# Mixer B's weighted products on GpSimd's queue: their places in a written-out plan and the tiles that they use, and one more tile for the sample's near keys

## Chip, core and metric

The kernel runs on one core of a Trainium2 chip. The metric is the device time of one execution in microseconds (us); given is the median of several runs. One further execution was recorded by the hardware profiler.

## What is computed

One step of a one-layer hybrid decoder, for a prompt of 1024 tokens and a sample group of 8 sequences with 4 new tokens each (32 rows). A normed input is projected into three mixers and their gates. Mixer A is sliding-window attention with sinks. Mixer B is attention in three groups of heads with dilations 1, 4 and 16; the three group outputs of a head slot are added, each weighted by its share of the softmax denominators:

```python
w_mix = jax.nn.softmax(jnp.stack(lses), axis=0)
ob = jnp.sum(w_mix[..., None] * jnp.stack(outs), axis=0)
```

Mixer C is a causal pooling over windows of 2, 4, 8 and 16 positions, followed by a small linear map. Each mixer's output is multiplied by a SiLU gate, projected to 1024 columns, merged by three sigmoid gates, passed through one output projection and added to the residual. The sample group does the same against key/value states of up to 2048 rows, which are inputs.

## The kernel before, in words

Everything is float32, computed as pairs of float32r numbers (a high and a low part), so each projection is three matmuls per tile of 128 input rows. TensorE runs the 58 column blocks of the input projection one after the other (`project`, L332). A block is three chunks of columns (384, 384 and 288 tokens), a chunk is 24 matmuls (L320), and after every 6 matmuls `tick` (L203) is called, so a block has 12 ticks. A chunk ends with the evacuation of its PSUM bank by ScalarE and VectorE; there are three such banks (`pj`).

All other work is hung on the ticks. A *plan* (`planned`, L219) is a list of (tick, function); at tick n all functions with that number emit their instructions. The *side* generators are advanced by a rate per tick. A tick orders instructions on each engine's queue, nothing more: an engine runs its queue in order, as soon as semaphores allow. The compiler framework hands out the buffers of a tag in the order of the first writes and adds all the waits.

The stage of this change follows the last block of the attention stage. Eight blocks (L1171 to L1176) project the gates of mixers C (t1c), B (t1_4, t1_5) and A (t1_0 to t1_3), 96 ticks. Beside them run, by `merge_plan` (L1155 to L1163):

- the weights of mixer B's groups (`stats_b`, L638): loaded into the tile `rows`, computed on VectorE, and written to DRAM (`w_scr`, L668) at tick 8;
- the pooling (`pooling`, L904): running sums (`window`) on GpSimd for the first half of the channels and on VectorE for the second, results `sa` and `sbb` in the tags l2 to l5; `body` and `small` (VectorE) turn them into `diff` in the tags df0 and df1; then `mix`, `times` and `parts_of` (ticks 22 to 39);
- mixer B's weighted products, six of them (pair p of 0, 1; group g of 0, 1, 2). Each is a load of the group's output from DRAM (`get_o`, L1118, 512 KB), two loads that spread the weights over 64 partitions each (`get_w`, L1126, 256 KB each), a product (`scale_o`, L1131), and for the second and third group a sum (`add_o`, L1136). All of these are issued from GpSimd's queue (POOL). After three groups `gate_b` (L1142, VectorE) multiplies the gate of the pair by the sum.

At ticks 48, 60, 72 and 84 the gates t1_0 to t1_3 are to be written to l2, l3, l4 and l5; their first chunk's evacuation comes four ticks later.

The sample group's attention (`sample`, L677) is a side generator. It issues its loads on SyncE's queue (SP): near keys and values into the tag `near` (two buffers, L683), far keys and values into the tag `kv` (five buffers, L711), which `rows` shares. Score steps t = 0 to 4 (L746 near, L765 far), then probabilities `probs` into tiles `pm` and `pd` (cleared by GpSimd, L802 and L804, at tick 41; filled by VectorE, L817, L822), then products with the values (L829, L852, L880). L774 and L829 are the new rows' small matmuls. The copies of the sample states in DRAM (L182) are issued on GpSimd's queue from tick 96 on.

```python
(44, get_b(1, 0, "l4")), (44, get_bw(1, 0, "l5")), (49, gate_b(0, (0, 0))),
...
(60, get_b(1, 2, "l3")), (60, get_bw(1, 2, "l5")), (67, scale_b(1, 2)), (67, add_o((1, 0), (1, 2))), (73, gate_b(1, (1, 0)))]
```

Of the kernel before, what the change touches and what calls it, by code (L numbers as in the profile page):

```python
# [7 lines left out]
F32 = mybir.dt.float32  # L8
# [7 lines left out]
L = 1024  # L16
# [80 lines left out]
def build(tc, x_p, x_s, w_in, w_pr, w_out, nw, fnw, sink, sinkrow, w_pool, pscale, st_a, st_b1, st_b2, st_b3, st_c,  # L97
# [579 lines left out]
    def sample(pl, ahead):  # L677
# [4 lines left out]
        def load_near(src):  # L682
            t = pl.tile([128, 8, 128], F32, tag="near", name="near", bufs=2)  # L683
            sp.dma_start(out=t, in_=src)
            near.append(t)

        load_near(kt_a)
        load_near(kt_b1[:, 0])
        qn = pl.tile([128, 10, 2, 32], F32, name="qn")
        pool.memset(qn, 0.0)  # L690
        for hh in range(2):
# [44 lines left out]
        for t in range(5):  # L736
            ps = bank("s")
            if t < 3:
                yield from idle(1)
                for nq in range(4):  # L740
                    for half in range(2):
                        n = 4 * half + nq
                        for p in range(2):
                            r0 = 64 * p + 32 * half
                            rhs = near[0 if t < 2 else 1 + p][:, n, :]
                            pe.matmul(ps[r0:r0 + 32, 0:128], lhsT=qm[:, 2 * t + p, half, 32 * nq:32 * nq + 32], rhs=rhs,  # L746
                                      start=(nq == 0), stop=(nq == 3))
            else:
                g = t - 2
                q_t = qd[0]  # L750
                for hh in range(2):
                    hs = slice(64 * hh, 64 * hh + 64)
                    dve.tensor_copy(out=q_t[hs].rearrange("p a b c -> p (a b) c")[:, :, 16 * hh:16 * hh + 496:33],
                                    in_=qsmp[hs, 2 * t:2 * t + 2].rearrange("p a (b t) -> p (a b) t", b=2))
                yield from idle(4)
                for nq in range(4):
                    yield from idle(4)
                    for i in range(4):
                        for half in range(2):
                            n = 4 * half + nq  # L760
                            kk = kv_tiles["k", g, n].rearrange("p (i a j) -> p i a j", i=4, a=2)
                            t16 = 4 * nq + i
                            for p in range(2):
                                r0 = 64 * p + 32 * half
                                pe.matmul(ps[r0:r0 + 32, 0:128], lhsT=q_t[:, p, half, 32 * t16:32 * t16 + 32], rhs=kk[:, i, p, :],  # L765
                                          start=(t16 == 0), stop=(t16 == 15))
                    load_ahead(4 * (g - 1) + nq + 2)
                    if nq < 3:
                        yield
            for half in range(2):  # L770
                for p in range(2):
                    r0 = 64 * p + 32 * half
                    ki = 0 if t < 2 else 2 * t - 3 + p
                    pe.matmul(ps[r0:r0 + 32, 128:160], lhsT=qn[:, 2 * t + p, half, :], rhs=ksmp[:, ki, :], start=True, stop=True)  # L774
            init = nsinkrow[:, t:t + 1] if t < 2 else 3.0e38
            dve.tensor_tensor_reduce(out=es[t], in0=ps[:, 0:160], in1=sb[:, t, :], scale=1.0, scalar=init, op0=ALU.add, op1=ALU.min,
                                     accum_out=st[:, t:t + 1])
            act.activation(out=es[t], in_=es[t], func=AF.Exp, scale=-1.0, bias=st[:, t:t + 1], accum_out=st[:, 8 + t:9 + t])
            if t < 2:
                act.activation(out=st[:, 16 + t:17 + t], in_=st[:, t:t + 1], func=AF.Exp, bias=sinkrow_sb[:, t:t + 1])  # L780
                dve.tensor_tensor(out=st[:, 16 + t:17 + t], in0=st[:, 16 + t:17 + t], in1=st[:, 8 + t:9 + t], op=ALU.add)
                dve.reciprocal(out=st[:, 16 + t:17 + t], in_=st[:, 16 + t:17 + t])
                dve.tensor_scalar(out=es[t], in0=es[t], scalar1=st[:, 16 + t:17 + t], scalar2=None, op0=ALU.mult)
            if t == 1:
                load_near(kt_b1[:, 1])
            if t == 2:
                load_near(st_a[:, 1].rearrange("n k c -> k n c"))
                load_near(st_b1[:, 1, :, 0:128].rearrange("n k c -> k n c"))
            yield
        dve.tensor_tensor(out=st[:, 24:25], in0=st[:, 2:3], in1=st[:, 3:4], op=ALU.min)  # L790
# [113 lines left out]
    def pooling(pl, up, oc, sa, sbb, after):  # L904
# [16 lines left out]
        def window(t, eng, dst, src, sh, base, hs=slice(0, 128)):  # L921
            def run():
                eng.tensor_tensor(out=dst[hs, base:n], in0=src[hs, base:n], in1=src[hs, base - sh:n - sh], op=ALU.add)
            return run

        def body(t, hh):
            hs, s = ((slice(0, 64), sa[t]), (slice(64, 128), sbb[t]))[hh]

            def run():
                dve.scalar_tensor_tensor(out=diff[t][hs, 16:L], in0=s[hs, 32:16 + L], scalar=pw_sb[hs, t, 16:17], in1=up[t][hs, 32:16 + L],  # L930
                                         op0=ALU.mult, op1=ALU.subtract)
                dve.tensor_tensor(out=diff[t][hs, 0:16], in0=s[hs, 16:32], in1=pw_sb[hs, t, 0:16], op=ALU.mult)
                dve.tensor_tensor(out=diff[t][hs, 0:16], in0=diff[t][hs, 0:16], in1=up[t][hs, 16:32], op=ALU.subtract)
            return run
# [4 lines left out]
        def small(t):  # L939
            def run():  # L940
                e = ext[:, t]
                dve.tensor_copy(out=e[:, :, 16:20], in_=usmp[:, t, :].rearrange("p (n i) -> p n i", i=4))
                win_s(ea, e, 1, 2)
                if t == 0:
                    win_s(eb, ea, 2, 4, slice(64, 128))
                else:
                    win_s(eb, ea, 2, 4)
                    win_s(ea, eb, 4, 8)
                    win_s(eb, ea, 8, 16, slice(64, 128))
                for hs, s in ((slice(0, 64), ea), (slice(64, 128), eb)):  # L950
                    dve.scalar_tensor_tensor(out=diff[t][hs, L:NT].rearrange("p (n i) -> p n i", i=4), in0=s[hs, :, 16:20],
                                             scalar=pw_sb[hs, t, 16:17], in1=e[hs, :, 16:20], op0=ALU.mult, op1=ALU.subtract)
            return run
# [27 lines left out]
        def parts_of(t):  # L981
            def run():
# [3 lines left out]

        h = slice(64, 128)
        out = [(0, setup), (1, window(0, pool, sa[0], up[0], 1, 1)), (2, window(0, pool, sbb[0], sa[0], 2, 3, h)),
               (9, window(1, dve, sa[1], up[1], 1, 1)), (11, window(1, dve, sbb[1], sa[1], 2, 3)),
               (13, window(1, dve, sa[1], sbb[1], 4, 7)), (15, window(1, dve, sbb[1], sa[1], 8, 15, h)),  # L990
               (16, body(0, 0)), (18, body(0, 1)), (19, small(0)), (20, body(1, 0)), (22, body(1, 1)), (23, small(1)),
               (30, rows_u(0)), (32, rows_u(1)), (33, times(0)), (35, parts_of(0)), (37, times(1)), (39, parts_of(1))]
        out += [(22 + 2 * ci, mix(0, c0, cn)) for ci, (c0, cn) in enumerate(CH)]
        out += [(28 + 2 * ci, mix(1, c0, cn)) for ci, (c0, cn) in enumerate(CH)]
# [139 lines left out]
    def add_o(a, b):  # L1134
        def run():
            pool.tensor_tensor(out=t_s[a][:, :L], in0=t_s[a][:, :L], in1=t_s[b][:, :L], op=ALU.add)  # L1136
        return run

    def gate_b(p, key):
        def run():  # L1140
            g = t1[4 + p][:, :L].rearrange("p (u r) -> p r u", r=8)
            dve.tensor_tensor(out=g, in0=g, in1=t_s[key][:, :L].rearrange("p (r u) -> p r u", r=8), op=ALU.mult)  # L1142
        return run

    def get_b(p, g, tag):
        return get_o((p, g), gl, tag, 4 + 2 * g + p)

    def get_bw(p, g, tag):
        return get_w((p, g, "w"), gl, tag, w_scr[g], 16 * p)

    def scale_b(p, g):
        return scale_o((p, g), (p, g, "w"))

# [1 line left out]
    merge_plan = stats_b(s1)  # L1155
    merge_plan += pooling(s1, up, oc, sa, sbb, (lambda: None, lambda: None))
    merge_plan += [
        (20, get_b(0, 0, "l2")), (20, get_bw(0, 0, "l3")), (27, scale_b(0, 0)),
        (28, get_b(0, 2, "l4")), (28, get_bw(0, 2, "l5")), (35, scale_b(0, 2)), (35, add_o((0, 0), (0, 2))),
        (36, get_b(0, 1, "l3")), (36, get_bw(0, 1, "l5")), (43, scale_b(0, 1)), (43, add_o((0, 0), (0, 1))),  # L1160
        (44, get_b(1, 0, "l4")), (44, get_bw(1, 0, "l5")), (49, gate_b(0, (0, 0))),
        (51, scale_b(1, 0)), (52, get_b(1, 1, "l3")), (52, get_bw(1, 1, "l5")), (59, scale_b(1, 1)), (59, add_o((1, 0), (1, 1))),
        (60, get_b(1, 2, "l3")), (60, get_bw(1, 2, "l5")), (67, scale_b(1, 2)), (67, add_o((1, 0), (1, 2))), (73, gate_b(1, (1, 0)))]  # L1163

    ahead = []
    smp = sample(s1, ahead)
# [351 lines left out]
```

## Time and profile before

| | us |
|---|---|
| median of 3 runs | 1084.41 (1084.41 to 1086.29) |
| profiled execution, its own time | 1083.06 |
| span of the profiled execution, first to last instruction | 1081.3 |
| TensorE busy / VectorE / ScalarE / GpSimd | 1040.3 / 433.1 / 346.6 / 215.1 |
| mean granted TensorE clock (1 is 2.4 GHz) | 0.987 |

The stage runs from about 448 to 598 us of the span. In the rows, PE is TensorE, PEld its weight loads, DVE VectorE, ACT ScalarE, POOL GpSimd, SP SyncE; "SPq", "POOLq" and "ACTq" are their queues when they issue a transfer. L12 is line 12 of the kernel.

### The profile page before, as it was taken

To read this page: it belongs to the slowest core of one execution; us is meant where nothing else is said; L and a number is where in the kernel's file an instruction comes from. 1 tells how busy PE (TensorE), PEld (TensorE's weight loads), DVE (VectorE), ACT (ScalarE), POOL (GpSimd) and SP (SyncE) were. 2 spreads that over 40 slices of the span, in tenths; PEclk is the share of its full clock that TensorE was granted. 3 is DMA by queue.
4 is the path that set the end of the run, shared out by engine and by line. 5 is a ranking of instruction groups with operands and counts; after the bars stand their busy time and mean duration, and the time that the engine had idled before them with its cause. 6 is when DMAs were issued, how large, how long until landed. Compare 5 with 4: busy or idle time off the path is not lost.

```text
span 1081.3 us, 18059 instructions
## 1 busy us (share of the span) xinstructions
PE 1040.3 (96%) x7421; PEld 992.5 (92%) x7421; DVE 433.1 (40%) x952; ACT 346.6 (32%) x890; POOL 215.1 (20%) x325
## 2 busy tenths in 40 slices
PE   7999999999999999999949999999999999999995
PEld 6998999999999999989939999999999999998884
DVE  6556654544535343475412551212112221255331
ACT  5455553544535344323201321211111121243211
POOL 5400030211303030305440340311113111121011
PEclk9999999999999999999979999999999999999998
DMA  7241242525344363488763823544234250332231
GB/s 262 87 152 57 65 132 85 168 69 174 102 156 144 111 192 100 142 269 287 212 210 105 259 98 107 177 145 136 77 118 150 65 172 20 113 112 93 79 100 41
DMA packets 54573, 144.41 MB, mean 134 GB/s; under 512 B 13030, under 2 KB 29732, under 8 KB 53156
## 3 DMA queue, kind: packets, MB, share of 16 engines
q1 hardware_dynamic: 40044, 58.94, 17.2%
q0 software_dynamic: 4640, 51.16, 14.3%
q10 hardware_dynamic: 9808, 33.17, 9.6%
q8 instruction: 58, 0.95, 0.4%
q14 instruction: 23, 0.19, 0.1%
HBM read 127.65 MB, written 60.55 MB: 174 GB/s over the span
## 4 chain that ended last, share of the span: by engine, by line
PE 84%; DMA 7%; DVE 3%; POOL 3%; ACT 2%; issue 1%; POOLq 0%; SPq 0%; ACTq 0%
PE ps_pj L320 55%; PE ps_pj L1389 5%; DMA w_in<-w_scr 5%; PE ps_s L1389 4%; PE ps_s L1254 4%; PE ps_t L1254 4%; PE ps_s L519 3%; PE ps_o L561 3%; PE ps_t L539 2%; POOL o_in L1131 1%; DMA w_raw<-in_w_in 1%; POOL o_in L1136 1%; DMA x_nat<-in_x_p 1%; PE ps_t L456 1%; DVE sq L295 1%
## 5 line engine op out<-in xcount | busy, mean ns | idle before, releaser
L320 PE MATMUL ps_pj<-xh,w_hi 128*128 128x384 f32 (+2 forms) x1408 | 461.0, 334 | 18.0 <-DVE t L1104 15.3
L320 PE MATMUL ps_pj<-xl,w_hi 128*128 128x384 f32 (+2 forms) x1408 | 444.8, 323 | 0.3 <-DVE xl L309 0.3
L320 PE MATMUL ps_pj<-xh,w_lo 128*128 128x384 f32 (+2 forms) x1408 | 443.4, 321 | 0.6 <-DVE w_lo L150 0.6
L320 PEld LDWEIGHTS ps_pj<-xh,w_hi 128*128 128x128 f32 x1408 | 262.5, 189 | 27.4 <-DVE t L1104 15.5
L320 PEld LDWEIGHTS ps_pj<-xl,w_hi 128*128 128x128 f32 x1408 | 263.0, 190 | 1.0 <-DVE xl L309 0.5
L320 PEld LDWEIGHTS ps_pj<-xh,w_lo 128*128 128x128 f32 x1408 | 261.8, 189 | 1.0 <-DVE w_lo L150 1.0
L150 DVE TENSOR_TENSOR w_lo<-w_raw,w_hi 128x1024 fp32r<-128x1024 f32 x55 | 73.7, 1339 | 203.0 <-ACT w_hi L149 202.6
L1263 ACT ACTIVATE mth<-ps_pj 128x384 f32<-128x384 f32 (+1 forms) x72 | 33.4, 464 | 255.0 <-PE ps_pj L320 252.3
L1271 POOL TENSOR_TENSOR m<-m,mth 128x384 f32<-128x384 f32 (+1 forms) x48 | 48.7, 1032 | 284.3 <-DVE mth L1269 284.0
L411 POOL TENSOR_SCALAR k<-k 64x384 fp32r<-64x384 f32 (+1 forms) x44 | 20.1, 458 | 297.5 <-ACT k L407 297.1
L526 ACT ACTIVATE e<-e,nm_b 128x256 f32<-128x256 f32 (+1 forms) x96 | 44.2, 461 | 63.1 <-DVE nm_b L523 62.8
L149 ACT ACTIVATE w_hi<-w_raw 128x1024 fp32r<-128x1024 f32 x57 | 60.1, 1054 | 0.8 <-DMA w_raw<-in_w_in 0.8
L371 DVE SCALAR_TENSOR_TENSOR q<-ps_pj,q 64x384 fp32r<-64x384 f32 (+1 forms) x60 | 30.7, 512 | 60.3 <-ACT q L370 60.2
L519 PE MATMUL ps_s<-k,q 128*128 128x256 f32 x320 | 51.6, 285 | 0.7 <-DVE nm_a L523 0.7
L519 PEld LDWEIGHTS ps_s<-k,q 128*128 128x128 f32 x320 | 45.9, 188 | 1.1 <-issue 1.0
L539 PE MATMUL ps_t<-ident,e 128*128 128x128 f32 x276 | 42.8, 273 | 1.8 <-ACT pt L544 1.1
L370 ACT ACTIVATE q<-ps_pj 64x384 fp32r<-64x384 f32 (+1 forms) x60 | 26.8, 447 | 50.4 <-PE ps_pj L320 29.3
L182 POOL DMA_DIRECT2D out_b_s<-in_st_b x84 | 42.2, 507 | 0.0
L526 ACT ACTIVATE e<-e,nm_a 128x256 f32<-128x256 f32 (+1 forms) x64 | 31.1, 487 | 28.1 <-DVE nm_a L523 28.1
L523 DVE CUSTOM_DVE_ANT_0 e<-ps_s,bias 128x256 f32<-128x256 f32 (+1 forms) x96 | 31.9, 371 | 14.9 <-PE ps_s L519 14.3
L539 PEld LDWEIGHTS ps_t<-ident,e 128*128 128x128 f32 x276 | 33.9, 140 | 4.1 <-ACT pt L544 1.7
L408 DVE TENSOR_TENSOR k<-ps_pj,k 64x384 fp32r<-64x384 f32 (+1 forms) x44 | 21.7, 494 | 38.7 <-ACT k L407 35.3
(243 smaller groups left out, 1337.5 us busy)
## 6 DMA issues: line engine op xcount, KB each, us to landing
out_b_s<-in_st_b POOLq DMA_DIRECT2D x64, 511.0 KB, 6.7
w_raw<-in_w_in ACTq DMA_DIRECT2D x55, 512.0 KB
kv<-in_kt_b SPq DMA_DIRECT2D x16, 512.0 KB
kv<-in_st_b SPq DMA_DIRECT2D x16, 512.0 KB
out_b_s<-in_st_b POOLq DMA_DIRECT2D x16, 508.0 KB, 5.2
o_scr<-os SPq DMA_DIRECT2D x20, 256.0 KB
x_nat<-in_x_p SPq DMA_DIRECT2D x8, 512.0 KB
w_raw<-in_w_pr ACTq DMA_DIRECT2D x8, 512.0 KB
```

The source lines that it names most:

```text
L149: act.activation(out=hi, in_=raw, func=AF.Copy)
L150: eng.tensor_tensor(out=lo, in0=raw, in1=hi.bitcast(F32), op=ALU.subtract)
L182: pool.dma_start(out=dst, in_=src)
L320: pe.matmul(ps[:, :cn], lhsT=parts[p][0][:, k, :], rhs=parts[p][1][:, k, c0:c0 + cn], start=(step == 0), stop=(step == 23))
L519: pe.matmul(ps[:, 256 * hd:256 * hd + 256], lhsT=q, rhs=rhs, start=(i == 0), stop=(i == 1))
L526: act.activation(out=e[:, hd, :nk], in_=e[:, hd, :nk], func=AF.Exp, scale=-1.0, bias=nm, accum_out=z)
L539: pe.transpose(tp[:, o:o + 128], e[:, hd, 128 * k:128 * k + 128], ident)
L561: pe.matmul(ps[64 * hd:64 * hd + 64, c0:c0 + 128], lhsT=v[:, tl, 64 * hd:64 * hd + 64], rhs=pt[:, o:o + 128], start=(k == 0), stop=(k == n ...
L1254: pe.matmul(pp[:, :cn], lhsT=a[:, k, :], rhs=b[k][:, c0:c0 + cn], start=(step == 0), stop=(step == last))
L1263: act.activation(out=th[:, :cn], in_=ps[:, :cn], func=AF.Tanh, scale=0.5)
L1271: pool.tensor_tensor(out=dst, in0=dst, in1=th[:, :cn], op=ALU.add)
L1389: pe.matmul(banks[c0][:rows, :cn], lhsT=a[:, k, t0:t0 + rows], rhs=wo[k][b][:, c0:c0 + cn], start=(k == 0 and si == 0), stop=(k == 7 and s ...
```

## The change

The products get other places in the plan: the first at tick 12 instead of 20, and the plan's last entry at 63 instead of 73. Within pair 0 the groups come in the order 0, 1, 2. A third product's load is under way while a second one waits for its weights, and the second and third products of pair 1 use the tags df0 and df1, which `parts_of` frees at ticks 35 and 39. `body` of the first half of the channels moves ahead of the running sums of the second. The third near-key tile no longer waits for one of the two near buffers: it takes a buffer of the tag `kv` and is loaded with the first two. The near values' loads move: st_a to t == 1, the first half of st_b1 to t == 3.

```diff
         load_near(kt_a)
         load_near(kt_b1[:, 0])
+        third = pl.tile([128, 16 + L], F32, tag="kv", name="near3", bufs=5)[:, :1024].rearrange("p (n k) -> p n k", n=8)
+        sp.dma_start(out=third, in_=kt_b1[:, 1])
+        near.append(third)
...
             if t == 1:
-                load_near(kt_b1[:, 1])
-            if t == 2:
                 load_near(st_a[:, 1].rearrange("n k c -> k n c"))
+            if t == 3:
                 load_near(st_b1[:, 1, :, 0:128].rearrange("n k c -> k n c"))
...
-               (9, window(1, dve, sa[1], up[1], 1, 1)), (11, window(1, dve, sbb[1], sa[1], 2, 3)),
-               (13, window(1, dve, sa[1], sbb[1], 4, 7)), (15, window(1, dve, sbb[1], sa[1], 8, 15, h)),
-               (16, body(0, 0)), (18, body(0, 1)), (19, small(0)), (20, body(1, 0)), (22, body(1, 1)), (23, small(1)),
+               (9, body(0, 0)), (11, body(0, 1)), (12, window(1, dve, sa[1], up[1], 1, 1)), (13, window(1, dve, sbb[1], sa[1], 2, 3)),
+               (14, window(1, dve, sa[1], sbb[1], 4, 7)), (16, window(1, dve, sbb[1], sa[1], 8, 15, h)),
+               (17, small(0)), (18, body(1, 0)), (20, body(1, 1)), (22, small(1)),
...
+    def get_d(p, g, t):
+        return get_o((p, g), s1, f"df{t}", 4 + 2 * g + p)
+
+    def get_dw(p, g, t):
+        return get_w((p, g, "w"), s1, f"df{t}", w_scr[g], 16 * p)
...
-        (20, get_b(0, 0, "l2")), (20, get_bw(0, 0, "l3")), (27, scale_b(0, 0)),
-        (28, get_b(0, 2, "l4")), (28, get_bw(0, 2, "l5")), (35, scale_b(0, 2)), (35, add_o((0, 0), (0, 2))),
-        (36, get_b(0, 1, "l3")), (36, get_bw(0, 1, "l5")), (43, scale_b(0, 1)), (43, add_o((0, 0), (0, 1))),
-        (44, get_b(1, 0, "l4")), (44, get_bw(1, 0, "l5")), (49, gate_b(0, (0, 0))),
-        (51, scale_b(1, 0)), (52, get_b(1, 1, "l3")), (52, get_bw(1, 1, "l5")), (59, scale_b(1, 1)), (59, add_o((1, 0), (1, 1))),
-        (60, get_b(1, 2, "l3")), (60, get_bw(1, 2, "l5")), (67, scale_b(1, 2)), (67, add_o((1, 0), (1, 2))), (73, gate_b(1, (1, 0)))]
+        (12, get_b(0, 0, "l2")), (12, get_bw(0, 0, "l3")), (20, scale_b(0, 0)),
+        (21, get_b(0, 1, "l3")), (22, get_bw(0, 1, "l4")), (30, scale_b(0, 1)), (30, add_o((0, 0), (0, 1))),
+        (23, get_b(0, 2, "l5")), (31, get_bw(0, 2, "l4")), (37, scale_b(0, 2)), (37, add_o((0, 0), (0, 2))), (43, gate_b(0, (0, 0))),
+        (38, get_b(1, 0, "l5")), (38, get_bw(1, 0, "l4")), (46, scale_b(1, 0)),
+        (40, get_d(1, 1, 0)), (40, get_dw(1, 1, 1)), (48, scale_b(1, 1)), (48, add_o((1, 0), (1, 1))),
+        (49, get_d(1, 2, 0)), (49, get_dw(1, 2, 1)), (57, scale_b(1, 2)), (57, add_o((1, 0), (1, 2))), (63, gate_b(1, (1, 0)))]
```

## Rows read from the trace of the kernel before

**Rows 1.** The page's granted clock in 40 slices of 27 us, tenths of full speed.

```profile
PEclk9999999999999999999979999999999999999998
```

**Rows 2.** Waits of PE, 440 to 640 us: us in total, times, longest.

```profile
PE ps_pj L320 <- DVE t L1104: 15.3, 1, 15.3
PE ps_s L746 <- DMA near<-in_kt_b: 2.5, 1, 2.5
```

**Rows 3.** The chain that ended last, 546 to 573 us: start, us, what.

```profile
546.97 12.22 DMA w_in<-w_scr
...
559.35 2.34 POOL o_in L1131
...
561.76 2.35 POOL o_in L1136
...
564.14 0.50 ACT t L1103
...
564.66 0.57 DVE t L1104
...
565.27 4.99 PE ps_pj L320 x18
```

**Rows 4.** Stretches: us; busy (count) of PE, PEld, DVE, ACT, POOL; clock, DMA share, GB/s.

```profile
460.00:465.00 5.00, 2.51 (x42) 2.26 (x41) 0.81 (x5) 0.05 (x1) 0.00 (x0) 0.79 0.30 99
465.00:470.00 5.00, 5.00 (x33) 5.00 (x32) 3.94 (x9) 1.35 (x5) 0.00 (x0) 0.87 0.85 277
...
565.00:570.00 5.00, 4.73 (x18) 4.67 (x18) 4.59 (x7) 1.38 (x4) 0.10 (x1) 0.63 0.89 314
```

**Rows 5.** Timeline of SP's queue, 446 to 460 us: start, us, instruction.

```profile
446.25 0.43 SPq L684 DMA_DIRECT2D near<-in_kt_b  x1
...
458.59 0.36 SPq L684 DMA_DIRECT2D near<-in_kt_b  x1
```

**Rows 6.** Timeline of PE, sample's matmuls.

```profile
462.67 1.53 PE L746 MATMUL ps_s<-near,qm 128*32 128x128 f32 x27 [2.49 <-DMA near<-in_kt_b]
...
476.21 1.08 PE L765 MATMUL ps_s<-kv,qd 128*32 128x128 f32 x32
...
520.91 0.42 PE L829 MATMUL ps_o<-vnat,pn 32*32 32x128 f32 x8
```

**Rows 7.** Timeline of ACT's queue (first row) and of DVE.

```profile
469.10 0.35 ACTq L668 DMA_DIRECT2D w_scr<-rows  x1
...
469.48 1.24 DVE L923 TENSOR_TENSOR pool_s<-up 128x1039 f32<-128x1039 f32 x1
...
476.38 1.25 DVE L930 SCALAR_TENSOR_TENSOR diff<-pool_s,pw_sb,up 64x1008 f32<-64x1008 f32 x1
...
514.80 0.36 DVE L817 COPY pm<-ps_t 128x64 f32<-128x64 f32 x2 [0.15 <-ACT pn L812]
...
524.67 2.28 DVE L1142 TENSOR_TENSOR t<-t,o_in 128x1024 f32<-128x1024 f32 x1 [2.29 <-POOL o_in L1136]
```

**Rows 8.** Timeline of POOL, 478 to 565 us.

```profile
478.29 0.61 POOL L1118 DMA_DIRECT2D o_in<-o_scr  x1 [22.64 <-issue]
479.59 1.06 POOL L1126 DMA_DIRECT2D w_in<-w_scr  x2 [0.69 <-DVE diff L933]
...
503.20 3.28 POOL L1136 TENSOR_TENSOR o_in<-o_in 128x1024 f32<-128x1024 f32 x1
...
508.04 0.98 POOL L802 MEMSET pm<- 128x1024 f32 x1
510.87 1.81 POOL L804 MEMSET pd<- 128x2048 f32 x1 [1.85 <-PE ps_s L774]
...
564.04 1.05 POOL L182 DMA_DIRECT2D out_b_s<-in_st_b  x2
```

**Rows 9.** Issues from POOL's queue: count, KB each, median us to landing.

```profile
w_in<-w_scr POOLq DMA_DIRECT2D x12, 256.0 KB, 7.5
```

**Rows 10.** Landing of the weights' loads, issues of 493 to 506 us alone.

```profile
DMA to landing us min/median/max: 5.5/5.6/5.6
```

## The prediction

> **What bounds the kernel now.** I read the clock line of the page first: one slice of forty is below full speed [rows 1], so something stops TensorE long enough there to slow it. The waits of PE over the stage say what: it waits only twice, 15.3 us for an evacuation of a projection and 2.5 us for a near-key load [rows 2]. The chain of waits shows what is behind the 15.3 us, in order: a load of the spread weights that takes 12.22 us to land, GpSimd's product and sum (2.34 and 2.35 us), then ScalarE's and VectorE's evacuation, then PE [rows 3]. This is the last product of mixer B. The gate t1_1 is to go to the tile l3, which that product still uses, so its first chunk cannot leave PSUM; PE fills the other banks and stands from 550.0 (565.27 less 15.3) to 565.27. Both waits cost a second time: PE's clock is at 1.2 instead of 2.4 GHz for a while afterwards. The stretches give it: after the near wait means of 0.79 and 0.87 over 5 us each, (0.21 + 0.13) x 5 = 1.7 us lost; after the long one 0.63, 0.37 x 5 = 1.85, less half of the 0.27 us before PE resumes, 1.7 us [rows 4]. So the two waits hold 15.3 + 1.7 + 2.5 + 1.7 = 21.2 us. Elsewhere in the stage PE is never short of work, so only these two matter.
>
> **The near-key tile.** Its load is issued at 458.59, when step t == 1 gives a buffer back, and PE gets it at 462.67: 4.1 us [rows 5, 6]. Now it is issued right behind the second near tile, at about 446.7. That is 13 us before PE comes for it, so the 2.5 + 1.7 us go. On SP's queue it is moved past the first far keys and the tile `rows`, which land up to one such load later (bounds 0 and 4.1 us); `rows` is read at about 457, ten us after its issue, and feeds only the weights. I take 0 for PE. st_a takes the old place of the near tile, st_b1's half comes behind the far keys of t == 3, long before its use after 520. From here on everything that PE paces is 4.2 us earlier.
>
> **Where the products start.** The first load now follows `body` of the first channels, which takes the place of the running sum at 469.48. Two bodies of some 1.6 us (1.25 and two small operations, taken as 0.35) end at 472.7, or up to 4.2 us earlier. The weights leave for DRAM at 469.10 less up to 4.2 and must have landed (4.1 us, as the near load). I take 471 for the first issue of the weights' loads, against 479.59 before [rows 7, 8]. The VectorE operations are the same ones in another order: 0, covered by the spare banks.
>
> **The chain of products.** Prices: issue of a group's load 0.6 us, of the two weights' loads 0.5 to the start of the second; landing 7.5 us, the median of twelve [rows 8, 9], with ends 5.5 (an undisturbed pair) and 12.2 (beside other loads) [rows 3, 10]; an operation on GpSimd 2.8, between 2.34 and 3.28 [rows 3, 8].
>
> Pair 0: 471 + 0.5 + 7.5 = 479.0, product 481.8; issues and landing (0.6 + 0.5 + 7.5) 490.4, product and sum 496.0; the third group is there already, its weights 504.0, product and sum 509.6. With the low ends 501.3, with the high ones 526.1.
>
> Pair 1: two groups' loads are issued at once, 2 x (0.61 + 1.06) = 3.3 us. The first lands at 509.6 + 1.1 + 7.5 = 518.2, product 521.0, the second has landed by then, product and sum 526.6, the last group 535.2, product and sum 540.8. High ends: 569.2. df1 is free at about 507 (`parts_of` at 511 less 4.2), no wait.
>
> **What waits for it.** Two points, both from rows less 4.2 us. First, `gate_b` of pair 0 is now at tick 43, ahead of the copies into `pm`; and GpSimd's clearing of `pm`, at tick 41, now stands behind the sum of pair 0 and the four issues. PE needs `pm` at 520.91 - 4.2 = 516.7; back over the copies (0.36), the clearing (0.98) and the issues (3.3), the sum must end by 512.0 (by `gate_b`, 2.28 us, by 514.0) [rows 6 to 8]. It ends at 509.6. Second, `gate_b` of pair 1 at tick 63 stands ahead of the evacuation for which PE would run out of banks at 550.0 - 4.2 = 545.8; back over 2.28 + 0.50 + 0.57, the last sum must end by 542.4 [rows 3, 7]. It ends at 540.8, where before it ended at 564.1. Both hold, by some 2 us. The gates t1_0 to t1_3 find their tiles free long before.
>
> Behind the last sum on GpSimd's queue stand two copies of states, at 564.04 [rows 8]; they move to about 541, beside the far values' loads, which go out as their buffers come free. Cost 0 to 2.8 us (half a landing of 5.5, if they share evenly), taken as 0, since these loads run two steps ahead of PE. After the stage nothing changes, so the gain reaches the end.
>
> **Sum.** 1083.06 - 21.2 = 1061.9 for the profiled execution. The median of the runs is 1.35 us above it, so 1063.2, forecast 1063.
>
> **Rivals.** *Later loads, slower than before.* The place is POOL's queue ahead of `pm`, and `gate_b` on DVE's. The price is the landing: with 12.2 and 3.28 pair 0 is 526.1 - 512.0 = 14.1 late, pair 1 another 569.2 - (542.4 + 14.1) = 12.7, two falls of the clock cost 3.4, in all 30.2 against 21.2 won: 1092 in the profile, 1093 in the median. The end moves 6 us for each us of landing, so it turns to a loss from a mean of about 10.7. For it: the first products now run while the far keys load, and 12.22 was seen beside the far values. Against: the median is 7.5. The Trainium skill's page "DMA: Bandwidth & Descriptors", section "Issuing engines are not separate DMA queues", says that transfers of all queues run on the same 16 DMA engines and interleave. By that rule two loads in flight win no bandwidth, and the time is the 1093 of this rival if SP's loads fill those engines throughout; the 12.22 against 5.5 us agrees with it where SP loads run beside. Chance 0.10.
>
> *A little late.* Landings of 9, or all operations at 3.28 (ten in the chain, 10 x 0.48 = 4.8 us): the last sum ends at 549.9 or 545.6, PE waits 7.5 or 3.2 us and loses 1.7 more (twice for the first): 1074 or 1068. For it: both points have only 2 us to spare. The Trainium skill's page "SBUF — State Buffer", section "Who interferes with whom", says that a VectorE operation with two SBUF inputs shuts out a GpSimd operation that reads SBUF. This would make the 3.28 us and the 1068 the rule beside VectorE's pooling; the 3.28 against 2.34 agrees. Chance 0.23.
>
> *The far ring runs short.* The near tile holds one of five `kv` buffers, so the next far key (needed at 476.21 - 4.2 = 472.0 [rows 6]) gets either the near tile's buffer, free at about 461, or that of `rows`, free when the weights have left, at about 471. In the second case it lands at 475 and PE waits 3 us and loses 1.7: 1068. Chance 0.08.
>
> *It doesn't do it.* If t1_1 were released by something other than the product, the wait would stay, 1080 to 1084. The chain names the sum directly before ScalarE. Chance 0.04.
>
> **Numbers.** The forecast has 0.55, on 1060 to 1066. The range 1060 to 1079 takes in the near-ring case, the late cases but the worst, and a clock that costs 2 us more than I took; it leaves out the slow rival and the one that does nothing. A change under 0.2% (2 us) can't be told from none. Faster 0.55 + 0.23 + 0.08 = 0.86, same 0.04, slower 0.10.
>
> **What would show it.** Right: no wait of PE in the stage, a full clock in all 40 slices, the weights' first load at about 471, the sum of pair 0 before 512 and the last one before 542, `gate_b` twice without idle time ahead of it. Wrong: PE waiting at L829 or L852 for the copies into `pm`, POOL's clearing of `pm` after 515, L765 waiting for a far key, or L320 still waiting for L1104 behind L1142.

## The result and the profile after

The changed kernel takes 1065.49 us in the median of four runs (1065.24 to 1066.44) against 1084.41 beside it: 0.9826 of the time before, interval 0.9809 to 0.9843. It is faster by 18.9 us. The forecast was 1063, with a range of 1060 to 1079. The profiled execution took 1066.44 us, span 1064.7, against 1083.06 and 1081.3.

Where the time came from is read in the same order as before. The clock line of the page and, below it, all waits of PE from 430 to 640 us (us in total, times, longest), which answer to [rows 1] and [rows 2]:

```profile
PEclk9999999999999999999999999999999999999998
```

```profile
PE ps_s L768 <- DMA kv<-in_kt_b: 1.8, 3, 0.9
```

The slow slice is gone, and so are the 15.3 us at L320 and the 2.5 us for the near tile. A new wait is there, for far keys (L768 is L765 of before). The timeline of PE has its three places, two steps of the far keys (start, us, instruction, idle time before it and its releaser; for the middle row of [rows 6]):

```profile
479.07 1.07 PE L768 MATMUL ps_s<-kv,qd 128*32 128x128 f32 x28 [0.88 <-DMA kv<-in_kt_b]
...
509.02 0.41 PE L768 MATMUL ps_s<-kv,qd 128*32 128x128 f32 x4 [0.30 <-DMA kv<-in_kt_b]
510.09 0.96 PE L768 MATMUL ps_s<-kv,qd 128*32 128x128 f32 x26 [0.65 <-DMA kv<-in_kt_b]
```

The chain that ended last now passes through these loads in place of the weights' load of [rows 3]:

```profile
469.77 9.25 DMA kv<-in_kt_b
...
500.76 9.28 DMA kv<-in_kt_b
```

POOL's timeline shows the new order of the products (issues L1120 and L1128, product L1133, sum L1138; against [rows 8]):

```profile
469.76 0.62 POOL L1120 DMA_DIRECT2D o_in<-o_scr  x1 [12.23 <-issue]
471.06 1.06 POOL L1128 DMA_DIRECT2D w_in<-w_scr  x2 [0.68 <-DVE diff L935]
481.57 3.46 POOL L1133 TENSOR_TENSOR o_in<-o_in,w_in 128x1024 f32<-128x1024 f32 x1 [9.45 <-DMA w_in<-w_scr]
...
495.25 2.38 POOL L1133 TENSOR_TENSOR o_in<-o_in,w_in 128x1024 f32<-128x1024 f32 x1 [7.72 <-DMA w_in<-w_scr]
...
511.76 2.41 POOL L1138 TENSOR_TENSOR o_in<-o_in 128x1024 f32<-128x1024 f32 x1
...
517.67 0.98 POOL L804 MEMSET pm<- 128x1024 f32 x1
...
542.67 2.39 POOL L1133 TENSOR_TENSOR o_in<-o_in,w_in 128x1024 f32<-128x1024 f32 x1 [9.20 <-DMA w_in<-w_scr]
545.15 2.39 POOL L1138 TENSOR_TENSOR o_in<-o_in 128x1024 f32<-128x1024 f32 x1
547.48 1.06 POOL L182 DMA_DIRECT2D out_b_s<-in_st_b  x2
```

On DVE the two gates (L1144) and the copies into `pm` follow (for the last two rows of [rows 7]):

```profile
515.59 2.26 DVE L1144 TENSOR_TENSOR t<-t,o_in 128x1024 f32<-128x1024 f32 x1
518.69 0.36 DVE L819 COPY pm<-ps_t 128x64 f32<-128x64 f32 x2 [0.84 <-POOL pm L804]
...
547.58 2.18 DVE L1144 TENSOR_TENSOR t<-t,o_in 128x1024 f32<-128x1024 f32 x1 [11.54 <-POOL o_in L1138]
549.66 0.99 DVE L1106 SCALAR_TENSOR_TENSOR t<-t,ps_pj 128x384 f32<-128x384 f32 x2
```

The last sum ends at 547.5 where it ended at 564.1. DVE stood 11.5 us ahead of the second gate, but PE lost nothing: it worked from the remaining banks. L1106 begins to empty the first at 549.66 (two operations in 0.99 us), and PE opens its next chunk at 550.25, so this held with some 0.1 us to spare.

The sum of the parts. I measure the stage on PE from its first transpose of the weights (L652) to the first matmul of the merge's projection: from 451.42 to 609.60 before (158.18 us), from 453.32 to 593.02 after (139.70). That is 18.48 us shorter. The stage also begins 1.90 us later in the profile of after, with the same program ahead of it; over all fourteen profiles of before, of after and of versions of both this beginning lies between 451.30 and 453.61, in no order of the versions (451.30 and 452.94 in two profiles of one kernel). So 1083.06 - 18.48 + 1.90 = 1066.48, measured 1066.44: nothing changes behind the stage.

### The profile page after: what moved, and what is told of

Its sections match the earlier page's. It is cut to its first block, busy times and chain, and to the rows that moved or that the text cites. A ratio compares the mean times of both kernels' runs of the same rounds, so it can differ in the third digit from the quotient of the medians.

```text
span 1064.7 us, 18072 instructions
## 1 busy us (share of the span) xinstructions
PE 1038.8 (98%) x7421; PEld 990.7 (93%) x7421; DVE 433.7 (41%) x952; ACT 347.0 (33%) x890; POOL 214.5 (20%) x325
## 4 chain that ended last, share of the span: by engine, by line
PE 90%; DMA 4%; DVE 2%; ACT 2%; issue 0%; POOL 0%; SPq 0%; POOLq 0%; ACTq 0%
PE ps_pj L320 60%; PE ps_pj L1397 5%; PE ps_s L1397 4%; PE ps_s L1262 4%; PE ps_t L1262 4%; PE ps_s L519 3%; PE ps_o L561 3%; PE ps_t L539 2%; DMA kv<-in_kt_b 2%; DMA w_raw<-in_w_in 1%; PE ps_o L882 1%; PE ps_s L768 1%; DVE sq L295 1%; DMA x_nat<-in_x_p 1%; PE ps_t L456 1%
## 5 line engine op out<-in xcount | busy, mean ns | idle before, releaser
L320 PE MATMUL ps_pj<-xh,w_hi 128*128 128x384 f32 (+2 forms) x1408 | 459.9, 333 | 3.0 <-ACT xh L308 3.0
L320 PE MATMUL ps_pj<-xl,w_hi 128*128 128x384 f32 (+2 forms) x1408 | 444.3, 322 | 0.3 <-DVE xl L309 0.3
L320 PE MATMUL ps_pj<-xh,w_lo 128*128 128x384 f32 (+2 forms) x1408 | 443.2, 321 | 0.7 <-DVE w_lo L150 0.7
L320 PEld LDWEIGHTS ps_pj<-xh,w_hi 128*128 128x128 f32 x1408 | 261.8, 189 | 12.2 <-issue 6.8
L320 PEld LDWEIGHTS ps_pj<-xl,w_hi 128*128 128x128 f32 x1408 | 262.5, 190 | 0.9 <-DVE xl L309 0.5
L320 PEld LDWEIGHTS ps_pj<-xh,w_lo 128*128 128x128 f32 x1408 | 261.6, 189 | 1.0 <-DVE w_lo L150 1.0
L150 DVE TENSOR_TENSOR w_lo<-w_raw,w_hi 128x1024 fp32r<-128x1024 f32 x55 | 69.1, 1256 | 201.6 <-ACT w_hi L149 201.4
L411 POOL TENSOR_SCALAR k<-k 64x384 fp32r<-64x384 f32 (+1 forms) x44 | 20.2, 460 | 299.1 <-ACT k L407 298.7
```

Of the source, the lines that this page charges most:

```text
L150: eng.tensor_tensor(out=lo, in0=raw, in1=hi.bitcast(F32), op=ALU.subtract)
L320: pe.matmul(ps[:, :cn], lhsT=parts[p][0][:, k, :], rhs=parts[p][1][:, k, c0:c0 + cn], start=(step == 0), stop=(step == 23))
```

## Experiments

All times are medians, with the ratio to the kernel before, run beside it, and its interval. "Plan" is the list of (tick, function) of the products. Waits of PE are always those of 430 to 640 us; the changed kernel's line numbers hold where those first two hunks are in, which move L765 to L768.

**1. The near tile alone.** The kernel before with the first two hunks of the diff only:

```diff
+        third = pl.tile([128, 16 + L], F32, tag="kv", name="near3", bufs=5)[...]
+        sp.dma_start(out=third, in_=kt_b1[:, 1])
...
             if t == 1:
-                load_near(kt_b1[:, 1])
-            if t == 2:
                 load_near(st_a[:, 1].rearrange("n k c -> k n c"))
```

> Before, with the near-key tile alone in the far ring (products, tiles and pooling's order as before). The forecast's term: 2.5 us of wait and 1.7 us of half clock go, so 4.2 us faster than before (ratio about 0.996), with the 15.3 us wait of L320 unchanged. Rival (the far ring runs short): a wait of L765 for a far key of 2 to 3 us takes the place of the near wait, ratio about 1.000. If the far keys' waits seen in the changed kernel (1.8 us in three pieces) come from the near tile's place in the ring, they are here too; if they come from the products' loads beside them, they are not.

1079.5 us, 0.9969 (0.9955 to 0.9982). Its waits of PE:

```profile
PE ps_pj L320 <- DVE t L1106: 15.8, 1, 15.8
PE ps_s L768 <- DVE qd L756: 0.4, 1, 0.4
```

The near wait is gone and the long one stands as it was. The part is worth 0.31% of 1084 = 3.4 us, for 2.5 + 1.7 = 4.2 in the sum, which lies inside the interval (2.0 to 4.9 us). No far key is waited for, so the tile in the far ring does not run it short by itself.

**2. The products alone.** The changed kernel without those two hunks.

> The changed kernel with the near-key load back in its old place. The near wait of 2.5 us and its half clock of 1.7 us return: about 4 us slower than the changed kernel, ratio to before about 0.986. If the far keys' waits come from the products' loads, some of them stay; if they come from the near tile in the ring, they are gone and it is only some 2.4 us slower than the changed kernel.

1068.62 us, 0.9861 (0.9839 to 0.9884). One wait of PE is left, the near tile's:

```profile
PE ps_s L746 <- DMA near<-in_kt_b: 2.2, 1, 2.2
```

No far key is waited for here either. The two parts add up: 3.4 and 15.1 (1.39% of 1084) make 18.5 of the 18.9 us.

**3. Of the products' part only the tiles.** The kernel before with its own start, order, spacing and gates; only the last two products of pair 1 go to df0 and df1:

```diff
-        (51, scale_b(1, 0)), (52, get_b(1, 1, "l3")), (52, get_bw(1, 1, "l5")), ...
-        (60, get_b(1, 2, "l3")), (60, get_bw(1, 2, "l5")), ...
+        (51, scale_b(1, 0)), (52, get_d(1, 1, 0)), (52, get_dw(1, 1, 1)), ...
+        (60, get_d(1, 2, 0)), (60, get_dw(1, 2, 1)), ...
```

> Before, with nothing changed but the tiles of the last two products (df0 and df1 instead of l3 and l5); start, order and spacing as before, so the last sum should still end near 564. Theory 'tile': PE stood only because t1_1's first chunk had to go to l3, which the sixth product still held; the multiplication of the gate stands ten ticks later, so PE does not stand: 15.3 + 1.7 = 17 us faster than before, ratio about 0.984, the near wait stays. Theory 'length': the end of the chain holds PE wherever its user stands; then no gain, ratio 1.000, and only an earlier or shorter chain helps.

1067.92 us, 0.9861 (0.9838 to 0.9884): the whole gain of experiment 2, with four edited entries of the plan. The stage is 17.3 us shorter than before (158.18 to 140.91), as the theory of the tile has it. The POOL and DVE timelines of this kernel show why it does not need the early start:

```profile
561.59 2.40 POOL L1136 TENSOR_TENSOR o_in<-o_in 128x1024 f32<-128x1024 f32 x1
```

```profile
552.50 0.45 DVE L1104 SCALAR_TENSOR_TENSOR t<-t,ps_pj 128x288 f32<-128x288 f32 x1 [0.53 <-ACT t L1103]
564.02 2.20 DVE L1142 TENSOR_TENSOR t<-t,o_in 128x1024 f32<-128x1024 f32 x1 [9.35 <-POOL o_in L1136]
566.84 1.02 DVE L1104 SCALAR_TENSOR_TENSOR t<-t,ps_pj 128x384 f32<-128x384 f32 x2 [0.62 <-ACT t L1103]
```

The last sum still ends at 564.0, as late as before, but nobody waits for it. The gate stands at tick 73, behind the three evacuations of t1_1, on the first of which PE stood before (here the third is at 552.50), and PE's only wait is the near tile's 2.3 us. What held PE before was the tile l3, which the last product shared with t1_1. The sum's time mattered through that alone. It could not end much later, though: the first of the two evacuations behind the gate is through at about 567.3, and PE opens its next chunk at 568.78.

**4. Spacing without the tiles.** The changed kernel with pair 1's second product in l3 and l4 at ticks 40 and 47, its third there at 55, products at 54 and 62.

```diff
-        (40, get_d(1, 1, 0)), (40, get_dw(1, 1, 1)), (48, scale_b(1, 1)), ...
-        (49, get_d(1, 2, 0)), (49, get_dw(1, 2, 1)), (57, scale_b(1, 2)), ...
+        (40, get_b(1, 1, "l3")), (47, get_bw(1, 1, "l4")), (54, scale_b(1, 1)), ...
+        (55, get_b(1, 2, "l3")), (55, get_bw(1, 2, "l4")), (62, scale_b(1, 2)), ...
```

> The changed kernel without df0 and df1: the last two products share l3 and l4 one after the other, the early start stays. Theory 'tile': t1_1's first chunk (tick 63, about 540) must wait for l3 until the last sum. The chain has one more landing in a row for pair 1 (about 7 us), so the last sum ends near 552 and L320 waits 3 to 8 us and loses some clock: 5 to 10 us slower than the changed kernel, ratio 0.987 to 0.992. Theory that the early start alone carries the gain: equal to the changed kernel, 0.983.

1072.05 us, 0.9909 (0.9883 to 0.9936). The stall at L320 is back in part, at the place in PE's timeline where the tile was the cause before:

```profile
554.20 0.69 PE L320 MATMUL ps_pj<-xh,w_hi 128*128 128x384 f32 x1 [4.98 <-DVE t L1106]
```

PE also waits 1.2 us at L854 for `pm`. So the early start without the tiles takes the stall from 15 to 5 us, and the tiles alone take all of it. What holds PE for the 5 us is not separated here: the last sum ends at 551.64, and at 551.67 two things begin that waited for it, ScalarE's part of the evacuation, which needs l3, and the gate, which at tick 63 stands ahead of VectorE's part (553.60). The gate's place by itself would give the same wait.

**5. The floor.** The changed kernel with no weighted product, sum or gate of mixer B in the plan.

> The changed kernel without mixer B's weighted products for the prompt: their loads, products, sums and the multiplication of the gate by them are left out, so this bounds what any plan for them can give. If the far keys' waits of 1.8 us come from the products' loads, L768 waits no more and it is about 2 us faster than the changed kernel, ratio to before about 0.981 (the forecast's full 21.2 us). If they come from the near tile in the ring, the waits stay and it equals the changed kernel, 0.983.

1060.7 us, 0.9794 (0.9771 to 0.9817), stage 20.2 us shorter than before. No far key is waited for; the only wait is 0.7 us for `qd`. All that the products still cost in the changed kernel is some 3.5 us (0.9826 less 0.9794, of 1084), a rough figure, since the two intervals overlap.

**6. The changed kernel again**, unchanged.

> The changed kernel once more, beside the same executions of before as the other kernels of this call: ratio 0.981 to 0.984, waits of L768 for far keys of about 1.8 us in the profile.

1065.2 us, 0.9844 (0.9818 to 0.987), but its six runs go from 1063.48 to 1071.65. The profiled one is the longest. Its waits, and the timeline of PE at the first of them:

```profile
PE ps_o L854 <- DVE pm L819: 3.9, 1, 3.9
PE ps_s L768 <- DMA kv<-in_kt_b: 2.0, 1, 2.0
PE ps_s L768 <- DVE qd L756: 0.3, 1, 0.3
```

```profile
525.44 1.14 PE L854 MATMUL ps_o<-near,pm 128*32 128x128 f32 x32 [3.89 <-DVE pm L819]
```

and POOL's timeline behind it:

```profile
515.58 2.37 POOL L1133 TENSOR_TENSOR o_in<-o_in,w_in 128x1024 f32<-128x1024 f32 x1 [11.37 <-DMA w_in<-w_scr]
518.03 2.40 POOL L1138 TENSOR_TENSOR o_in<-o_in 128x1024 f32<-128x1024 f32 x1
...
523.92 0.98 POOL L804 MEMSET pm<- 128x1024 f32 x1
```

Here the weights of pair 0's third product come 11.4 us after POOL is idle for them; its sum ends at 520.4 instead of 514.2, the clearing of `pm` behind it is 6 us later, and PE waits for the copies. This is the rival "a little late", at the first of its two points. It costs the wait and a slower clock behind it: a mean of 0.91 over the 20 us from 520.

**7. Tiles and near tile, nothing else.** Experiment 3 with the two hunks of experiment 1, measured twice.

> Before, with the last two products in df0 and df1 and the near-key tile in the far ring; start, order, spacing and the place of the gate's multiplication as before. Theory 'tile' (early start, spacing and two loads in flight are worth nothing, and the products' loads laid beside the far keys' loads cost 1.8 us): no wait of L768 for a far key, about 1.5 us faster than the changed kernel, ratio 0.980 to 0.982. Theory that the early start is needed once PE runs 4.2 us earlier: the last sum ends near 562, the multiplication holds VectorE, and L320 waits some us; then it is slower than the changed kernel.

> The kernel before with the two parts that carried the gain and nothing else (products (1,1) and (1,2) in the pooling's result tiles, the third near tile in the far ring). Theory: the early start costs the changed kernel some 2 us at L768, so this version is 1 to 3 us faster than the changed kernel beside it, 1061.5 to 1064.5, with a narrower spread of single runs (under 4 us) since both its deadlines have more to spare. Rival: the earlier difference of 2.3 us between the two was chance; both then lie within 1 us.

1062.94 us (0.9817, 0.9796 to 0.9837) the first time, 1066.01 (0.9827, 0.9804 to 0.985) the second time. The stretch 470 to 560 us of the first (us; busy and count of PE, PEld, DVE, ACT, POOL; clock, DMA share, GB/s) has PE busy without a gap:

```profile
470.00:560.00 90.00, 90.00 (x986) 81.07 (x984) 42.45 (x83) 19.85 (x41) 38.87 (x32) 1.00 0.85 272
```

Behind this stretch the gate is only just in time: the last sum ends at 559.17, the first evacuation behind the gate starts at 562.01, and PE opens its next chunk at 562.62 after 0.14 us without work. The profile of the second has two waits, both for far loads:

```profile
PE ps_s L768 <- DMA kv<-in_kt_b: 1.2, 1, 1.2
PE ps_o L882 <- DMA kv<-in_st_b: 1.0, 1, 1.0
```

The first measurement spoke for a cost of the early start, the second does not. All runs of each together give 1063.4 in the median (ten runs, 1061.8 to 1066.1) against 1065.5 for the changed kernel (fifteen, 1063.5 to 1071.7). The difference is 2.1 us, about what can be told from none, and the intervals of the ratios overlap. What is shown is that the early start, the spacing and the gates at 43 and 63 win nothing measurable over the two small parts.

**8. The changed kernel beside the second of these.**

> The changed kernel unchanged, once more, as the other side of three comparisons. Its earlier runs lay between 1063.5 and 1071.7 us. Theory: 1065 (1063 to 1067) in the median, with single runs up to 1072 in which the first deadline (the copies into pm ahead of L854) is missed; PE waits about 2 us at L768 for far keys in every profile. Rival: the 1071.7 was an accident of one chip, and no run here is above 1068.

1066.08 us, 0.9832 (0.9809 to 0.9854), no run above 1067. Its waits:

```profile
PE ps_o L854 <- DVE pm L819: 1.3, 1, 1.3
PE ps_s L768 <- DVE qd L756: 0.6, 1, 0.6
PE ps_s L768 <- DMA kv<-in_kt_b: 0.6, 1, 0.6
```

The forecast of single long runs failed here, but the first point is missed again, by 1.3 us.

**9. One product's loads at a time.** The changed kernel with the group of (0,2) loaded at 31 beside its weights, and (1,1) at 47:

```diff
-        (23, get_b(0, 2, "l5")), (31, get_bw(0, 2, "l4")), ...
+        (31, get_b(0, 2, "l5")), (31, get_bw(0, 2, "l4")), ...
-        (40, get_d(1, 1, 0)), (40, get_dw(1, 1, 1)), ...
+        (47, get_d(1, 1, 0)), (47, get_dw(1, 1, 1)), ...
```

> The changed kernel, in which the loads of product (0,2) go out together at step 31 and those of (1,1) at step 47, each after the product ahead of it, so that no second pair of loads is in flight. Theory: two loads in flight are worth nothing by themselves as long as a deadline isn't missed, but pair 0's third product gets later by the 3 to 4 us that a half-megabyte transfer takes beside another, and the first deadline had next to nothing to spare: PE waits 1 to 5 us at L854 for pm, 1066 to 1071. Rival: loads in flight together only share the same engines, the third product comes no later, and the time stays at 1065 plus or minus 1.

1074.5 us, 0.9916 (0.9886 to 0.9946), 8.4 us more than the changed kernel beside it (experiment 8), beyond what I expected and at another place. Waits of PE, the chain, and two stretches:

```profile
PE ps_s L768 <- DMA kv<-in_kt_b: 4.7, 3, 2.0
PE ps_pj L320 <- DVE t L1106: 2.2, 1, 2.2
```

```profile
500.61 11.80 DMA kv<-in_kt_b
```

```profile
510.00:515.00 5.00, 2.96 (x44) 2.60 (x45) 1.00 (x4) 0.55 (x3) 2.56 (x2) 0.81 1.00 330
515.00:520.00 5.00, 5.00 (x30) 4.95 (x29) 4.19 (x7) 1.28 (x5) 4.70 (x6) 0.84 0.49 165
```

The wait is not for `pm` but for the last far keys: they are issued at 500.1, and the product's megabyte (a group and two weights, instead of the two weights alone) leaves POOL's queue between 499.4 and 501.1. That load now lands in 11.80 us, against 9.28 in the changed kernel. Two waits of 1.75 and 1.96 us follow each other, and PE's clock falls to means of 0.81 and 0.84 for 10 us: (0.19 + 0.16) x 5 = 1.75 us more. Then the second pair is late. Its second product starts at 534.41 for 526.69: the first sum ends 3.0 us later (517.18 for 514.17), and the loads of (1,1) go out at 527.60 for 516.09, which is the other half of the edit. PE waits 2.2 us at L320 for the gate's sake, and its clock falls once more (means of 0.75 and 0.91 from 555 to 565, another 1.7 us). So within this plan the early loads do work: that of (0,2) keeps half a megabyte out of the last far keys' way, and that of (1,1) keeps the second gate in time. How the 8.4 us divide between the two was not measured by itself.

**10. `pm` cleared ahead of pair 1's first loads.** Pair 0's last product and its sum at tick 41, its gate at 46, pair 1's first loads at 42. Two entries that are not shown below move too: the sum of (1,1) from 48 to 49 and pair 1's gate from 63 to 66, behind the first evacuation of t1_1. The loads of (1,1), left at 40, now stand ahead of pair 0's last product.

```diff
-        ... (37, scale_b(0, 2)), (37, add_o((0, 0), (0, 2))), (43, gate_b(0, (0, 0))),
-        (38, get_b(1, 0, "l5")), (38, get_bw(1, 0, "l4")), (46, scale_b(1, 0)),
+        ... (41, scale_b(0, 2)), (41, add_o((0, 0), (0, 2))), (46, gate_b(0, (0, 0))),
+        (42, get_b(1, 0, "l5")), (42, get_bw(1, 0, "l4")), (49, scale_b(1, 0)),
```

> The changed kernel with pair 0's last product and sum four steps later (41), its gate at 46, pair 1's first loads at 42 and product at 49: on POOL the clearing of pm and pd then stands directly behind the sum, ahead of the first loads of pair 1, where it stood behind two pairs of issues (3.2 us). Theory: the misses of the first deadline (3.9 us at L854 in one profile) come from that order, so they go or shrink to under 1 us; the wait at L768 stays at about 2 us; median 1064 (1062.5 to 1066), no run above 1068. Rival: the misses come from late landings ahead of the sum and the order gives nothing: same times and spread as the changed kernel beside it; or pair 1's later loads miss the second deadline, PE waits for L1106, and it is 1 to 4 us slower.

1063.33 us (1062.16 to 1064.89), 0.9809 (0.9785 to 0.9833). POOL's timeline and PE's waits:

```profile
511.48 2.41 POOL L1138 TENSOR_TENSOR o_in<-o_in 128x1024 f32<-128x1024 f32 x1
513.82 0.96 POOL L804 MEMSET pm<- 128x1024 f32 x1
```

```profile
PE ps_s L768 <- DMA kv<-in_kt_b: 1.5, 3, 0.6
PE ps_s L768 <- DVE qd L756: 0.6, 1, 0.6
```

The clearing follows the sum at once; in the changed kernel 3.5 us lay between (514.17 to 517.67). The wait at L854 is gone, the one for far keys is not. All five runs lie under the median of 1065.5, but the intervals overlap: this is the best complete version of the study by its ratio, not one that is shown to beat the changed kernel. With the other moves in the edit, its gain, if there is one, can't be put down to the clearing alone.

**11. Far keys earlier.** The third far step's two tiles moved to the free tags l0 and l1 of the gates, in place of buffers of the ring:

```diff
+                if (what, g, nq) == ("k", 1, 2):
+                    t = gl.tile([128, NT], F32, tag=f"l{half}", name="kv")[:, :1024]
```

> The changed kernel with the two far-key tiles of the third step (whose late landing PE waited for) in l0 and l1, which are free until tick 27, so the far ring has two tiles less to carry and all later far loads go out two buffers earlier. If the 1.8 us are loads that go out too late for their slower landing beside the products' loads, the waits of L768 go and it is about 1.8 us faster than the changed kernel, ratio about 0.981. If the DMA engines are full, so that nothing lands earlier however early it is issued, the waits stay and it equals the changed kernel.

1066.35 us, 0.9838 (0.9815 to 0.9861): no gain. Neither place of the first profile's wait has one now, but a wait of the same size stands at another (L771 is L768 of the changed kernel):

```profile
505.54 1.86 PE L771 MATMUL ps_s<-kv,qd 128*32 128x128 f32 x28 [1.90 <-DMA kv<-in_kt_b]
```

The chain names its load, 10.15 us from 495.35. So buffers were not what these loads lacked.

## Why the prediction was right, and where its steps were not

- **Two waits and two falls of the clock hold 21.2 us.** Right in kind: all four are gone. The near part measured 3.4 for 4.2 us, and tiles and near tile without a wait of any size shorten the stage by 158.18 - 137.07 = 21.1 us in the first profile of experiment 7 (18.5 in the second, which has two waits for far loads).
- **The far ring costs nothing.** That is true of the tile by itself (experiment 1), and two more buffers leave a wait of the same size (experiment 11), so it is not the ring that runs short. The step that failed is "Elsewhere in the stage PE is never short of work", with "I take 0 for PE": the sum has no term for what the products' earlier loads do to the far keys. In the changed kernel the loads that PE waits for land in 9.3 us beside the products' loads, PE comes for the first of them some 4 us earlier, and waits 1.8 us in all (2.0 and 0.6 in the other two profiles). This differs between executions: experiment 4, with the same early loads, has no such wait in its profile, and the second profile of experiment 7, with the old start, has 1.2 us. Without products (experiment 5) or with PE 4 us later (experiment 2) none was seen. Of the 21.2 - 18.5 = 2.7 us missing from the stage, 1.8 is this wait. The other 0.9 fits the same steps, which keep PE busy for 1.1 us longer where waits break them up, while no other group of PE's instructions in the stage differs by more than 0.2; first the changed kernel, then the first profile of experiment 7 (busy us, mean ns of one, idle time before):

```profile
L768 PE MATMUL ps_s<-kv,qd 128*32 128x128 f32 x256 | 9.7, 276 | 1.8 <-DMA kv<-in_kt_b 1.8
L768 PE MATMUL ps_s<-kv,qd 128*32 128x128 f32 x256 | 8.6, 276 | 0.0
```

The remaining 1.9 us of the profile's miss is the stage's late beginning.
- **Start at 471.** The weights' first load was issued at 471.06, though with everything 1.9 us later.
- **The chain of products.** The prices were low where transfers meet: the weights landed in 8.6 us in the median, for 7.5.

```profile
w_in<-w_scr POOLq DMA_DIRECT2D x12, 256.0 KB, 8.6
```

Pair 0's sum ended at 514.2, 2.7 us after the forecast (509.6 + 1.9), the last one at 547.5, 4.8 us after it (540.8 + 1.9).
- **"Both hold, by some 2 us".** Not by the prediction's own sum. With the 1.9 us of late beginning, pair 0's sum was to end by 513.9 and ended at 514.2; the last one was to end by 544.3 and ended at 547.5. PE lost nothing in the first profile since it was late itself: it reached L831 at 521.30 for a forecast 516.7 + 1.9, the copies into `pm` having started at 518.69, and it came for the bank of the second point at 550.25 for a forecast 545.8 + 1.9. The way from the last sum to the first free bank was also shorter, 2.6 for 3.35 us. That both points held there is luck: without the 1.8 us of waits for far keys PE would, by these times, have waited about as long at the second point (worked out, not run). In the two other profiles the first point was missed by 3.9 and 1.3 us; the second held, by some 1.1 and 1.6 us. The range was made for this, and 0.23 for a rival that decides single executions was not too much.
- **The signs.** Of the prediction's list, the start of the weights' loads and the full clock came as right. The sums after 512 and 542, the 11.5 us of idle time ahead of the second gate, the clearing of `pm` after 515 (517.67) and the wait for far keys came as wrong. The time still lies near the forecast since these misses cost PE little, in part by the luck above.
- **The second point was made by the change.** I counted the last sum's end, 564.1 before and 547.5 now, as what the gain rests on. Experiment 3 shows that it rests on the tile: with the gate left at tick 73, a sum that ends at 564.0 costs nothing. By putting the gate at 63, ahead of an earlier evacuation, the change brought its deadline forward by 17.2 us (the evacuation behind the gate is at 566.84 there and at 549.66 here), about as much as the sum (564.1 to 547.5). The prediction read the tile rightly (t1_1 "is to go to the tile l3, which that product still uses"), named both edits and gave the tile no share of its own.
- **Later loads, slower.** Its mechanism is real: experiment 9 brings transfers together, delays the second pair and gives 8.4 us back, less than the 30.2 that I worked out for every landing at 12.2. The Trainium skill's page "DMA: Bandwidth & Descriptors", section "Issuing engines are not separate DMA queues", has all queues share the same 16 engines and interleave; the 11.80 us of a key load beside the megabyte, against 9.28 beside half of it (one profile each), agree. The turning point near a mean landing of 10.7 was not reached (8.6). It lies later by the prediction's own chain, which has five landings in a row and not six: at about 11.4, and with landings of 9 the last sum would end at 548.3, not 549.9 (1072, not 1074).
- **GpSimd's slow operations.** The first product took 3.46 us, with DVE busy for 9.09 of the 10 us around it, and 2.38 later. The Trainium skill's page "SBUF — State Buffer", section "Who interferes with whom", gives this cause; the rows agree, and the price of 2.8 us for an operation was high enough. VectorE paid as well: of two equal operations of 64x16 elements, the one that met this product (481.57 to 485.03) took 2.37 us for 0.16.

```profile
480.65 0.16 DVE L934 TENSOR_TENSOR diff<-pool_s,pw_sb 64x16 f32<-64x16 f32 x1
...
482.69 2.37 DVE L934 TENSOR_TENSOR diff<-pool_s,pw_sb 64x16 f32<-64x16 f32 x1
```

- **The state copies** moved to 547.48 and no wait is tied to them.

## What to carry to other kernels

When a chain ends in an evacuation that waits for a late product, first ask which resource joins the two: a buffer that is shared by order of first write can be given another name, and the late product may then be as late as it was, if its next user leaves it the time (in experiment 7 just so). Moving the product earlier won the same time here only by bringing new transfers beside others and by making new deadlines. A deadline that holds by 2 us behind loads whose landing goes from 5.5 to 12.2 us holds in some executions and not in others, so look at several runs, not at one trace.

## What was not expected of the hardware

- Executions of one program differ in the landing of one load by several us: the weights of pair 0's third product made POOL wait 8.21, 8.59 and 11.37 us in three profiles of the changed kernel. The longest wait, 3.2 us above the first, is half of the 6.2 us by which that sum came later (520.4 for 514.2); the other half was there when the load was issued (503.14 for 500.02).
- Issuing the loads of two products some 12 us later (499.41 for 486.95 and 527.60 for 516.09), which moves no byte more, costs 8.4 us here (1074.5 against 1066.1). In the profiles the last far keys then land in 11.80 instead of 9.28 us, the second gate is late, and PE's clock falls behind either wait.
